# The bias of a decay's exponent: direction 0's inside the exponential, head by head, direction 1's as a difference

## The chip, the cores and the metric

The kernel runs on one core of a Trainium2 chip. The metric is the time of one execution on the device in microseconds (us). Of the core's engines, TensorE (PE) does the matmuls and transposes, VectorE (DVE) the elementwise work on two operands, ScalarE (ACT) functions such as the exponential, GpSimd (POOL) some elementwise work, and the sync engine (SP) issues most of the transfers from memory. Each engine works its own queue of instructions in order.

## The reference, cut to what matters

The layer has two branches behind one input projection: gated linear attention (GLA) and a Mamba-2 scan (SSD), each run in both directions over 512 tokens, merged, and followed by a feed-forward part. The change is in the SSD branch: 32 heads in 4 groups, chunks of 128 tokens. Within a chunk the reference computes for each head

```python
cum = jnp.cumsum(ai, axis=1)
seg = cum[:, :, None] - cum[:, None, :]
Lm = jnp.exp(jnp.where(mask, seg, -jnp.inf))
cb = jnp.einsum('btgn,bsgn->btsg', ci, bi)
y = jnp.einsum('btsg,btsge,bsgep->btgep', cb, Lm, xi)
```

`seg` is the decay's exponent for the pair of tokens t and s, and `xi` is already multiplied by the step size dt. Direction 0 uses the pairs with s at or before t, direction 1 those with s at or after t.

## The kernel before

Each product with weights is made of three matmuls: high part by high part, high by low, low by high. ScalarE writes the high part of a weight tile (`whi_...`, L188) and VectorE the rest (`wlo_...`, L189) from a tile `raw_...` that the sync queue loads (L176).

The SSD branch goes group by group. `ssd_proj(g)` makes B, C, x and the gate z of a group; z comes last, in two halves of 256 columns into banks `r_z` (L386 to L388), and each bank is read by ScalarE (L697) and VectorE (L698) and then used again. `ssd_chain(g)` then runs over the group's four chunks n. The names count chunks (`y_3` is the matmul of chunk 3 of some group); `y_2` in VectorE's rows is the tile of y of group 2. For each chunk and each half of the group's eight heads (`hf`, four heads) the chain makes a tile E of 128 partitions (token s) by 4 x 128 (head, token t), named `E_n_hf_d` in the queue:

- two loads, one for each direction d, bring the row of cumulative sums `cdr` into all partitions (L746). The pool "E4" has four buffers, so two half-chunks are in flight at once.
- VectorE adds `ebias`, which is log dt minus the cumulative sum at s, one value for each partition and head, to each direction (L747).
- `copy_predicated` (L749) writes direction 0's values over direction 1's where s is at or before t.
- ScalarE takes the exponential of the tile (L750), VectorE multiplies it by the product of C and B (L757), and TensorE multiplies it with x into `y_3`.

The pieces of y are then added on VectorE: the contributions `yi` of the two carried states (L773, L774), the bank (L775), the gate z (L776). ScalarE sums the squares (L781), VectorE and GpSimd make the norm's factor (`rv_y`, `rr_y`), VectorE scales (L783). TensorE transposes the result (`yT_3`, L501), ScalarE and VectorE write its high and low part (L788, L789), and `pb` matmuls project it (L632 to L634). While the chain of group g runs, TensorE fills the time with the projections of group g+1, or, for the last group, with the gate projections `l_ga` and `l_gb`.

Nobody writes the order of the queues by hand: a scheduler replays the program by its own estimates of time and writes each engine's queue; matmuls issued through `early` (L501) have priority in it.

Of the kernel before, what the change touches and what calls it, by code (L numbers as in the profile page):

```python
# [11 lines left out]
AF = mybir.ActivationFunctionType  # L12
ALU = mybir.AluOpType

P = 128
# [12 lines left out]
HPG = 8  # L28
# [101 lines left out]
def hybrid_layer_kernel(ctx: ExitStack, tc: tile.TileContext, x, xc, wts, vec, rows, up, msk, lvl, out):  # L130
    nc = tc.nc
# [569 lines left out]
    def ssd_chain(g, bc, bt, xt, z, yH, yL):  # L701
# [35 lines left out]
        for n in range(NCH):  # L737
            tk = slice(n * P, (n + 1) * P)
            EH = HPG // 2
            Eh = []  # L740
            for hf in range(2):
                E = []
                hh = slice(g * HPG + hf * EH, g * HPG + (hf + 1) * EH)
                for d in range(2):
                    ed = ch.tile([P, EH, P], F32, tag="E4", name=f"E_{g}_{n}_{hf}_{d}", bufs=4)
                    nc.sync.dma_start(ed, cdr[d, n, hh, :].unsqueeze(0).to_broadcast([P, EH, P]))  # L746
                    nc.vector.tensor_tensor(ed, ed, ebias[:, d, n, hh].unsqueeze(2).to_broadcast([P, EH, P]), ALU.add)  # L747
                    E.append(ed)
                nc.vector.copy_predicated(E[1], le8.unsqueeze(1).to_broadcast([P, EH, P]), E[0])  # L749
                nc.scalar.activation(E[1], E[1], AF.Exp)  # L750
                Eh.append(E[1])
            pcb = sm_bank(f"cb_{g}_{n}")
            early.matmul(pcb[:, 0:P], bc[:, 0, tk], bc[:, 1, tk], start=True, stop=True)
# [116 lines left out]
    ebias = cst.tile([P, 2, 4, 32], F32, name="ebias")  # L870
    for d in range(2):
        nc.vector.tensor_tensor(ebias[:, d], ldt[:, 0:4, 32 * d:32 * d + 32], cum[:, d], ALU.subtract)
    cdr = dr.tile([2, 4, 32, P], F32, name="cdr")
    for d in range(2):
        pt = sm_bank(f"cumT_{d}")
# [18 lines left out]
    nc.gpsimd.dma_start(ydr, acc_a)  # L894
    yy = back_pair("yT_0")
    ssd_chain(0, *sp, *yy)
    acc_b = ch.tile([P, 8, SEQ], F32, tag="y16", name="acc_b")
    sp = ssd_proj(1)
    proj_back(lambda c: ("pb", 0, c), *yy, acc_b, True)
    yy = back_pair("yT_1")  # L900
    ssd_chain(1, *sp, *yy)
    sp = ssd_proj(2)
    proj_back(lambda c: ("pb", 1, c), *yy, acc_b, False)
    yy = back_pair("yT_2")
    ssd_chain(2, *sp, *yy)
    sp = ssd_proj(3)
    proj_back(lambda c: ("pb", 2, c), *yy, acc_b, False)
# [292 lines left out]
```

## Time and profile before

| | before |
|---|---|
| median of 3 runs | 1412.5 us (1412.01 to 1418.23) |
| profiled execution | 1415.85 us, of which the span in the trace is 1414.1 |
| mean granted clock of TensorE | 0.981 |
| busy: TensorE, VectorE, ScalarE, GpSimd | 1353.3, 871.4, 504.2, 331.7 us |
| chain that ended last | TensorE 80%, VectorE 9%, transfers 6%, ScalarE 2% |

The profiled execution is one of its own and lies 3.35 us above the median. A busy time says how long an engine had work in it; the chain says which work the end of the program waited for.

### The profile page before, as it was taken

Reading aid. Unit: us, or ns where it says so; the run is one execution under the profiler, and the core shown is the slowest. Engines: PE = TensorE matmul, PEld = TensorE weight load, DVE = VectorE, ACT = ScalarE, POOL = GpSimd, SP = SyncE. Lnnn points to the kernel's source line nnn. Section 1 sums busy time; section 2 is a strip of 40 time slices with the busy share of each in tenths; the row PEclk is TensorE's granted clock in tenths of the full one; section 3 lists DMA queues with packets and bytes.
Section 4 is the critical chain, followed back from the end, with each engine's and each line's share of the span. In section 5 each row is a group of like instructions: output and inputs, shape, how many; then the busy total and the mean of one; then the engine's idle time right before and its main releaser. Section 6 shows DMA issues by size and latency. Waiting matters only on the chain.

```text
span 1414.1 us, 19042 instructions
## 1 busy us (share of the span) xinstructions
PE 1353.3 (96%) x7462; PEld 1151.4 (81%) x7462; DVE 871.4 (62%) x1348; ACT 504.2 (36%) x828; POOL 331.7 (23%) x277
## 2 busy tenths in 40 slices
PE   5998999999999999999899989998899999999997
PEld 3797999899889788888878877776688888888886
DVE  4559686573786697678759865777664434332235
ACT  6474343433435232532423342232333232232222
POOL 1355454245001211111021102114641212100001
PEclk9899999999999999999999989999999999999999
DMA  9363322333222333223323233547423343333231
GB/s 367 131 211 105 103 94 94 123 105 123 94 83 90 122 118 103 85 89 93 109 75 103 94 92 96 175 155 252 152 77 119 104 134 120 123 100 104 90 112 67
DMA packets 58010, 169.19 MB, mean 120 GB/s; under 512 B 6064, under 2 KB 10304, under 8 KB 57792
## 3 DMA queue, kind: packets, MB, share of 16 engines
q1 hardware_dynamic: 55328, 157.96, 34.2%
q0 software_dynamic: 2304, 9.64, 2.2%
q8 instruction: 59, 0.97, 0.3%
q10 hardware_dynamic: 288, 0.36, 0.1%
q14 instruction: 31, 0.25, 0.1%
HBM read 156.23 MB, written 11.72 MB: 119 GB/s over the span
## 4 chain that ended last, share of the span: by engine, by line
PE 80%; DVE 9%; DMA 6%; ACT 2%; issue 2%; POOL 1%; SPq 0%; POOLq 0%; DVEq 0%; ACTq 0%
DMA E<-cdr 3%; PE up L1054 3%; PE gate L1053 3%; PE up L1053 3%; PE gate L1054 3%; PE gate L1052 3%; PE up L1052 3%; PE db L204 3%; PE db L206 3%; PE db L205 3%; PE yi L501 2%; PE l_xs L361 2%; PE l_xs L366 2%; PE l_xs L362 2%; PE pb_pb L632 2%; PE pb_pb L633 2%
## 5 line engine op out<-in xcount | busy, mean ns | idle before, releaser
L341 POOL TENSOR_TENSOR raw_ada<-raw_ada,cs 128x1024 f32<-128x1024 f32 x32 | 63.7, 1990 | 277.7 <-DMA raw_ada<-in_wts_dram 234.3
L386 PE MATMUL r_z<-whi_z,hH 128*128 128x256 f32 x256 | 75.6, 295 | 7.4 <-DVE z L698 6.8
L343 POOL TENSOR_TENSOR raw_ada<-raw_ada 128x512 f32<-128x512 f32 x64 | 80.1, 1251 | 4.3
L387 PE MATMUL r_z<-wlo_z,hH 128*128 128x256 f32 x256 | 75.6, 295 | 0.0
L388 PE MATMUL r_z<-whi_z,hL 128*128 128x256 f32 x256 | 74.6, 291 | 0.0
L1052 PE MATMUL gate<-h2H,whi_gate 128*128 128x512 f32 (+1 forms) x192 | 71.6, 373 | 0.3 <-ACT h2H L1023 0.2
L1053 PE MATMUL gate<-h2L,whi_gate 128*128 128x512 f32 (+1 forms) x192 | 71.5, 373 | 0.3 <-DVE h2L L1024 0.3
L747 DVE TENSOR_TENSOR E<-E,ebias 128x512 f32<-128x512 f32 x64 | 46.1, 724 | 41.3 <-DMA E<-cdr 41.0
L1054 PE MATMUL gate<-h2H,wlo_gate 128*128 128x512 f32 (+1 forms) x192 | 71.4, 372 | 0.0
L1054 PE MATMUL up<-h2H,wlo_up 128*128 128x512 f32 x160 | 63.0, 394 | 0.0
L1053 PE MATMUL up<-h2L,whi_up 128*128 128x512 f32 x160 | 62.3, 389 | 0.0
L1052 PE MATMUL up<-h2H,whi_up 128*128 128x512 f32 x160 | 62.2, 389 | 0.0
L189 DVE TENSOR_TENSOR wlo_gate<-raw_gate,whi_gate 128x1024 fp32r<-128x1024 f32 x20 | 33.4, 1672 | 45.2 <-ACT whi_gate L188 45.2
L189 DVE TENSOR_TENSOR wlo_down<-raw_down,whi_down 128x1024 fp32r<-128x1024 f32 x18 | 22.1, 1225 | 62.4 <-ACT whi_down L188 62.3
L386 PEld LDWEIGHTS r_z<-whi_z,hH 128*128 128x128 f32 x256 | 50.7, 198 | 8.4 <-DVE z L698 7.4
L386 PE MATMUL r_v<-whi_v,hH 128*128 128x256 f32 x192 | 55.7, 290 | 1.0 <-ACT whi_v L188 1.0
L205 PE MATMUL db<-wlo_down,fH 128*128 128x512 f32 x142 | 55.2, 389 | 0.0
L206 PE MATMUL db<-whi_down,fL 128*128 128x512 f32 x142 | 55.2, 389 | 0.0
L388 PE MATMUL r_v<-whi_v,hL 128*128 128x256 f32 x192 | 55.1, 287 | 0.0
L632 PE MATMUL pb_pb<-yT,whi_pb 128*128 128x512 f32 x128 | 53.3, 421 | 1.5 <-ACT z L697 1.0
L387 PE MATMUL r_v<-wlo_v,hH 128*128 128x256 f32 x192 | 54.6, 284 | 0.0
L633 PE MATMUL pb_pb<-yT,whi_pb 128*128 128x512 f32 x128 | 52.8, 413 | 1.5 <-DVE yT L789 1.5
(473 smaller groups left out, 4262.6 us busy)
## 6 DMA issues: line engine op xcount, KB each, us to landing
raw_ada<-in_wts_dram SPq DMA_DIRECT2D x32, 512.0 KB, 3.6
E<-cdr SPq DMA_DIRECT2D x64, 256.0 KB, 3.2
raw_gate<-in_wts_dram SPq DMA_DIRECT2D x22, 512.0 KB, 3.6
raw_up<-in_wts_dram SPq DMA_DIRECT2D x22, 512.0 KB, 3.6
raw_down<-in_wts_dram SPq DMA_DIRECT2D x22, 512.0 KB, 3.6
aw<-in_wts_dram SPq DMA_DIRECT2D x8, 1024.0 KB, 15.5
raw_xs<-in_wts_dram SPq DMA_DIRECT2D x16, 512.0 KB, 3.5
raw_z<-in_wts_dram SPq DMA_DIRECT2D x16, 512.0 KB, 3.5
```

Source lines behind the costliest of these rows:

```text
L205: nc.tensor.matmul(out_, aH, bL, start=False, stop=False)
L206: nc.tensor.matmul(out_, aL, bH, start=False, stop=stop)
L341: nc.gpsimd.tensor_tensor(raw, raw, cs[:, :, 0:1].to_broadcast([P, KD, P]), ALU.mult)
L343: nc.gpsimd.tensor_tensor(raw[:, 0:n, :], raw[:, 0:n, :], raw[:, n:2 * n, :], ALU.add)
L386: nc.tensor.matmul(o, hH[:, kk, tk], hi[:, k, :], start=st, stop=False, skip_group_check=True)
L387: nc.tensor.matmul(o, hH[:, kk, tk], lo[:, k, :], start=False, stop=False, skip_group_check=True)
L388: nc.tensor.matmul(o, hL[:, kk, tk], hi[:, k, :], start=False, stop=sp, skip_group_check=True)
L632: nc.tensor.matmul(pt, hi[:, k, cl], aH[:, k, :], start=(k == 0), stop=False)
L633: nc.tensor.matmul(pt, hi[:, k, cl], aL[:, k, :], start=False, stop=False)
L1052: nc.tensor.matmul(pts[kj][:, tk], hi[:, k, :], h2H[:, k, tk], start=(k == 0), stop=False)
L1053: nc.tensor.matmul(pts[kj][:, tk], hi[:, k, :], h2L[:, k, tk], start=False, stop=False)
L1054: nc.tensor.matmul(pts[kj][:, tk], lo[:, k, :], h2H[:, k, tk], start=False, stop=(k == KD - 1))
```

## The change

Direction 0's add is left out. Its bias is put into the exponential instead, where ScalarE can add one value for each partition; as the value differs from head to head, the one instruction over four heads becomes four over one head each. Direction 1's add stays, but adds the difference of the two biases, so that the exponential's bias completes both. The table of differences is made once, after `ebias` is set up.

```diff
--- before.py
+++ after.py
@@ -744,10 +744,13 @@
                 for d in range(2):
                     ed = ch.tile([P, EH, P], F32, tag="E4", name=f"E_{g}_{n}_{hf}_{d}", bufs=4)
                     nc.sync.dma_start(ed, cdr[d, n, hh, :].unsqueeze(0).to_broadcast([P, EH, P]))
-                    nc.vector.tensor_tensor(ed, ed, ebias[:, d, n, hh].unsqueeze(2).to_broadcast([P, EH, P]), ALU.add)
+                    if d == 1:
+                        nc.vector.tensor_tensor(ed, ed, ebias[:, 1, n, hh].unsqueeze(2).to_broadcast([P, EH, P]), ALU.add)
                     E.append(ed)
                 nc.vector.copy_predicated(E[1], le8.unsqueeze(1).to_broadcast([P, EH, P]), E[0])
-                nc.scalar.activation(E[1], E[1], AF.Exp)
+                for e_ in range(EH):
+                    b_ = g * HPG + hf * EH + e_
+                    nc.scalar.activation(E[1][:, e_, :], E[1][:, e_, :], AF.Exp, bias=ebias[:, 0, n, b_:b_ + 1])
                 Eh.append(E[1])
             pcb = sm_bank(f"cb_{g}_{n}")
             early.matmul(pcb[:, 0:P], bc[:, 0, tk], bc[:, 1, tk], start=True, stop=True)
@@ -870,6 +873,8 @@
     ebias = cst.tile([P, 2, 4, 32], F32, name="ebias")
     for d in range(2):
         nc.vector.tensor_tensor(ebias[:, d], ldt[:, 0:4, 32 * d:32 * d + 32], cum[:, d], ALU.subtract)
+
+    nc.vector.tensor_tensor(ebias[:, 1], ebias[:, 1], ebias[:, 0], ALU.subtract)
     cdr = dr.tile([2, 4, 32, P], F32, name="cdr")
     for d in range(2):
         pt = sm_bank(f"cumT_{d}")
```

TensorE keeps its instructions; the scheduler writes all queues anew. Three places follow, each a piece of an engine's queue. A number behind a name only tells tiles of one name apart, `x3` is three alike in a row, and [waits ...] names the engine or transfer queue whose count the instruction waits for (Activation is ScalarE, DMAHW a transfer).

TensorE before, where the chain of group 2 ends and the gate z of group 3 is projected, up to the first `pb` matmul:

```order
L386 MATMUL r_z_1_0_1_7551<-whi_z_1_1_7606,hH 128x256
L387 MATMUL r_z_1_0_1_7551<-wlo_z_1_1_7607,hH 128x256
L388 MATMUL r_z_1_0_1_7551<-whi_z_1_1_7606,hL 128x256
L501 MATMUL yT_3_6988<-idt,y_2_6967 128x128 [waits DVE_49,PE_49]
L501 MATMUL yT_3_6988<-idt,y_2_6967 128x128 x3
L674 MATMUL tr_b_0_7066<-idt,ct_b_7061 128x128 [waits PE_49]
L674 MATMUL tr_b_0_7066<-idt,ct_b_7061 128x128 x3
L674 MATMUL tr_b_1_7072<-idt,ct_b_7061 128x128 [waits PE_49]
L674 MATMUL tr_b_1_7072<-idt,ct_b_7061 128x128
L674 MATMUL tr_x_0_0_7184<-idt,ct_x_0_7181 128x128 [waits PE_49,Activation_49]
L674 MATMUL tr_x_0_0_7184<-idt,ct_x_0_7181 128x128 x3
L632 MATMUL pb_pb_0_0_7674<-yT_6679,whi_pb_0_7668 128x512 [waits Activation_49]
```

TensorE in the change, at the same transposes:

```order
L386 MATMUL r_z_0_0_1_7482<-whi_z_0_1_7537,hH 128x256
L387 MATMUL r_z_0_0_1_7482<-wlo_z_0_1_7538,hH 128x256
L388 MATMUL r_z_0_0_1_7482<-whi_z_0_1_7537,hL 128x256
L501 MATMUL yT_3_7037<-idt,y_2_7016 128x128 [waits DVE_49,PE_49]
L501 MATMUL yT_3_7037<-idt,y_2_7016 128x128 x3
L674 MATMUL tr_b_0_7115<-idt,ct_b_7110 128x128 [waits PE_49]
L674 MATMUL tr_b_0_7115<-idt,ct_b_7110 128x128 x3
L674 MATMUL tr_b_1_7121<-idt,ct_b_7110 128x128 [waits PE_49]
L674 MATMUL tr_b_1_7121<-idt,ct_b_7110 128x128
L674 MATMUL tr_x_0_0_7233<-idt,ct_x_0_7230 128x128 [waits PE_49,Activation_49]
L674 MATMUL tr_x_0_0_7233<-idt,ct_x_0_7230 128x128 x3
L386 MATMUL r_z_1_0_0_7599<-whi_z_1_0_7601,hH 128x256 [waits DVE_49]
```

Before, 48 `r_z` matmuls of the second half of z stand between the last `y_3` and `yT_3`, and `pb` follows the transposes. In the change it is 44 `r_z` of the first half; the second half follows `yT_3` and the transposes, and the first `pb` comes 118 instructions behind `yT_3`. The queue reads the same at the ends of groups 0 and 1, where 64 and 75 instructions stood between the last `y_3` and `yT_3` before; at the end of group 1 the first matmul of the second half (`r_z_1_0_0`) came right behind the last `y_3` and waited for z. At the end of group 3 there are 40 matmuls of 512 columns (`l_ga`, `l_gb`) in that place, and before there were 9.

VectorE before, at the same end of group 2, from the second piece of y to its scaling in L783:

```order
L747 TENSOR_TENSOR E_0_1_1_7858<-E_0_1_1_7858,ebias 128x512 [waits DMAHW6_49]
L774 TENSOR_TENSOR y_2_6967<-y_2_6967,yi_2_6976 128x512 [waits DVE_49]
L749 COPY_PREDICATED E_0_1_1_7858<-le_78,E_0_1_0_7855 128x512 [waits DVE_49]
L775 TENSOR_TENSOR y_2_6967<-y_2_6967,y_3_6958 128x512 [waits DVE_49,PE_49]
L747 TENSOR_TENSOR E_1_0_0_7917<-E_1_0_0_7917,ebias 128x512 [waits DMAHW7_49]
L776 TENSOR_TENSOR y_2_6967<-y_2_6967,z_3_6306 128x512 [waits DVE_49]
L189 TENSOR_TENSOR wlo_pb_0_7669<-raw_pb_0_7670,whi_pb_0_7668 128x1024 [waits Activation_49]
L747 TENSOR_TENSOR E_1_0_1_7920<-E_1_0_1_7920,ebias 128x512 [waits DMAHW0_49]
L168 TENSOR_SCALAR rv_y_6983<-yss_3_6981 128x1 [waits Activation_49]
L698 SCALAR_TENSOR_TENSOR z_3_7431<-z_3_7431,r_z_0_0_1_7433 128x256 [waits DVE_49,Activation_49]
L749 COPY_PREDICATED E_1_0_1_7920<-le_78,E_1_0_0_7917 128x512 [waits DVE_49]
L783 SCALAR_TENSOR_TENSOR y_2_6967<-y_2_6967,rr_y_6985,snw_6680 128x512 [waits Pool_49]
```

VectorE in the change, from the first piece of y to its scaling, which is L786 there (pieces are L776 to L779, the add is L748, the copy L750):

```order
L776 TENSOR_TENSOR yi_2_7020<-yi_3_0_7018,ecum 128x512 [waits PE_49]
L776 TENSOR_TENSOR yi_2_7025<-yi_3_1_7023,ecum 128x512 [waits PE_49]
L777 TENSOR_TENSOR y_2_7016<-y_2_7016,yi_2_7020 128x512 [waits DVE_49,Pool_49]
L777 TENSOR_TENSOR y_2_7016<-y_2_7016,yi_2_7025 128x512 [waits DVE_49]
L778 TENSOR_TENSOR y_2_7016<-y_2_7016,y_3_7007 128x512 [waits DVE_49,PE_49]
L748 TENSOR_TENSOR E_0_1_1_7908<-E_0_1_1_7908,ebias 128x512 [waits DMAHW5_49]
L779 TENSOR_TENSOR y_2_7016<-y_2_7016,z_3_6339 128x512 [waits DVE_49]
L750 COPY_PREDICATED E_0_1_1_7908<-le_78,E_0_1_0_7906 128x512 [waits DMAHW2_49,DVE_49]
L698 SCALAR_TENSOR_TENSOR z_0_7477<-z_0_7477,r_z_0_0_0_7481 128x256 [waits Activation_49]
L168 TENSOR_SCALAR rv_y_7032<-yss_3_7030 128x1 [waits Activation_49]
L786 SCALAR_TENSOR_TENSOR y_2_7016<-y_2_7016,rr_y_7034,snw_6713 128x512 [waits Pool_49]
```

Ahead of y's scaling stand one E add, one copy, one piece of z and `rv_y` now; the add of `E_1_0_0` is gone, and the weight split and the add of `E_1_0_1` come later.

The sync queue before, some way ahead of that place (`raw_` tiles are weights, E tiles the rows of `cdr`):

```order
L746 DMA E_3_0_1_6935<-cdr 128x512 [waits DVE_49]
L746 DMA E_3_1_0_6940<-cdr 128x512 [waits DMAHW5_49,DVE_49]
L176 DMA raw_z_1_1_7608<-in_wts_dram 128x1024 [waits DMAHW6_49,DVE_49]
L176 DMA raw_pb_0_7670<-in_wts_dram 128x1024 [waits DMAHW7_49,DMAHW0_49,DVE_49]
L746 DMA E_3_1_1_6943<-cdr 128x512 [waits DVE_49,PE_49]
L746 DMA E_0_0_0_7847<-cdr 128x512 [waits DMAHW1_49,DVE_49,PE_49]
L746 DMA E_0_0_1_7850<-cdr 128x512 [waits DMAHW2_49,DVE_49]
L176 DMA raw_pb_1_7704<-in_wts_dram 128x1024 [waits DMAHW3_49,DVE_49]
L746 DMA E_0_1_0_7855<-cdr 128x512 [waits DMAHW4_49,DVE_49]
```

The sync queue in the change at the same loads:

```order
L746 DMA E_3_1_0_6987<-cdr 128x512 [waits DMAHW4_49,DMAHW1_49,DVE_49]
L176 DMA raw_z_1_0_7603<-in_wts_dram 128x1024 [waits DMAHW6_49,DVE_49]
L746 DMA E_3_1_1_6989<-cdr 128x512 [waits DVE_49,PE_49]
L746 DMA E_0_0_0_7896<-cdr 128x512 [waits DMAHW7_49,DVE_49,PE_49]
L176 DMA raw_z_1_1_7657<-in_wts_dram 128x1024 [waits DMAHW0_49,DVE_49]
L746 DMA E_0_0_1_7898<-cdr 128x512 [waits DMAHW4_49,DVE_49]
L746 DMA E_0_1_0_7906<-cdr 128x512 [waits DMAHW7_49,DMAHW2_49,DVE_49]
L176 DMA raw_pb_0_7719<-in_wts_dram 128x1024 [waits DMAHW3_49,DVE_49]
L176 DMA raw_pb_1_7753<-in_wts_dram 128x1024 [waits DMAHW5_49,DVE_49]
```

`raw_z_1_1` and `raw_pb_0` now stand behind E loads that stood behind them before.

## Rows read from the trace of the kernel before

**Rows 1.** The page: busy time, share and instructions of TensorE; the chain that ended last.

```profile
PE 1353.3 (96%) x7462; PEld 1151.4 (81%) x7462; DVE 871.4 (62%) x1348; ACT 504.2 (36%) x828; POOL 331.7 (23%) x277
...
PE 80%; DVE 9%; DMA 6%; ACT 2%; issue 2%; POOL 1%; SPq 0%; POOLq 0%; DVEq 0%; ACTq 0%
```

**Rows 2.** Windows: length, busy us (instructions) by engine, TensorE's clock, DMA share, GB/s.

```profile
690.00:825.00 135.00, 129.37 (x739) 110.02 (x740) 100.16 (x164) 44.12 (x77) 19.36 (x17) 0.96 0.27 87
825.00:960.00 135.00, 124.55 (x561) 97.31 (x559) 90.83 (x139) 45.66 (x76) 22.03 (x23) 0.95 0.44 139
```

**Rows 3.** Windows of 10 us, the same columns.

```profile
690.00:700.00 10.00, 7.34 (x42) 7.34 (x43) 4.99 (x10) 4.04 (x9) 0.55 (x1) 0.66 0.22 57
...
810.00:820.00 10.00, 10.00 (x69) 9.52 (x68) 6.10 (x13) 2.33 (x6) 1.05 (x1) 0.83 0.25 79
830.00:840.00 10.00, 7.90 (x28) 6.39 (x29) 6.26 (x10) 5.69 (x11) 0.00 (x0) 0.57 0.50 151
...
960.00:970.00 10.00, 9.79 (x34) 7.94 (x35) 3.66 (x7) 1.74 (x3) 2.19 (x3) 0.78 0.81 290
```

**Rows 4.** Waits of TensorE, 400 to 960 us: total, times, longest.

```profile
PE yT L501 <- DVE y L783: 7.3, 2, 3.8
PE r_z L386 <- DVE z L698: 6.8, 3, 3.3
```

**Rows 5.** TensorE's timeline: start, duration, instruction, [idle before <- releaser].

```profile
562.44 0.39 PE L386 MATMUL r_z<-whi_z,hH 128*128 128x256 f32 x1 [1.58 <-DVE z L698]
562.66 0.28 PE L387 MATMUL r_z<-wlo_z,hH 128*128 128x256 f32 x1
...
692.66 0.58 PE L386 MATMUL r_z<-whi_z,hH 128*128 128x256 f32 x1 [3.27 <-DVE z L698]
693.04 0.41 PE L387 MATMUL r_z<-wlo_z,hH 128*128 128x256 f32 x1
693.26 0.41 PE L388 MATMUL r_z<-whi_z,hL 128*128 128x256 f32 x1
...
830.60 0.63 PE L501 MATMUL yT<-idt,y 128*128 128x128 f32 x4 [3.53 <-DVE y L783]
...
835.48 0.80 PE L633 MATMUL pb_pb<-yT,whi_pb 128*128 128x512 f32 x1 [1.50 <-DVE yT L789]
...
958.43 1.09 PE L501 MATMUL yT<-idt,y 128*128 128x128 f32 x4 [3.76 <-DVE y L783]
```

**Rows 6.** VectorE's timeline at the end of group 2.

```profile
822.93 0.69 DVE L747 TENSOR_TENSOR E<-E,ebias 128x512 f32<-128x512 f32 x1 [1.32 <-DMA E<-cdr]
...
825.36 0.69 DVE L747 TENSOR_TENSOR E<-E,ebias 128x512 f32<-128x512 f32 x1
...
826.59 1.23 DVE L189 TENSOR_TENSOR wlo_pb<-raw_pb,whi_pb 128x1024 fp32r<-128x1024 f32 x1
828.11 0.69 DVE L747 TENSOR_TENSOR E<-E,ebias 128x512 f32<-128x512 f32 x1 [0.28 <-DMA E<-cdr]
...
829.72 0.74 DVE L783 SCALAR_TENSOR_TENSOR y<-y,rr_y,snw 128x512 f32<-128x512 f32 x1
```

**Rows 7.** Groups: L747 (ns min/median/max, waits); ScalarE's, 400 to 960 us (busy, mean ns).

```profile
L747 DVE TENSOR_TENSOR E<-E,ebias x64: 670/693/1277, 412.5 to 934.7; 128x512 f32<-128x512 f32 x64
...
  DMA E<-cdr: 41.0, 39
...
L750 ACT ACTIVATE E<-E 128x512 f32<-128x512 f32 x32 | 20.2, 633 | 80.3 <-DVE E L749 75.6 <-DVE rv_y L168 4.7
...
L657 ACT ACTIVATE cv_x<-c_xs,vecs 128x256 f32<-128x256 f32 x15 | 8.3, 555 | 0.0
...
L675 ACT ACTIVATE x<-tr_x 128x256 f32<-128x256 f32 x16 | 6.2, 386 | 0.0
...
L755 ACT ACTIVATE cbs<-cb 128x128 f32<-128x128 f32 x16 | 4.4, 274 | 26.7 <-PE cb L501 26.7
```

**Rows 8.** Waits of the sync queue, 400 to 960 us.

```profile
SPq L746 <- DVE E L749: 91.9, 27, 6.5
```

## The prediction

> **What bounds the kernel now.** I read the page first: TensorE is busy for 96% of the span and the chain that ended last lies on it for 80%, with 9% on VectorE and 6% on transfers [rows 1]. A change that adds no matmul and takes none away can therefore move the time in two ways only: through the moments in which TensorE stands still, and through the clock at which it runs. So I read next, in two long stretches of the part that the change touches, those of the last two groups, TensorE's busy time and granted clock [rows 2]. From 690 to 825 us it misses 5.6 us of 135 and from 825 to 960 it misses 10.5, at a clock of 0.96 and 0.95. VectorE is busy for two thirds to three quarters of each stretch and ScalarE for a third: neither is full. So the loss sits in short places.
>
> The short windows find the places [rows 3]: four of ten microseconds run at 0.66, 0.83, 0.57 and 0.78. What that costs I take as the missing share of the clock times TensorE's busy time in the window: 0.34 × 7.34 = 2.5, 0.17 × 10 = 1.7, 0.43 × 7.9 = 3.4, 0.22 × 9.79 = 2.2, together 9.8 us. The waits by releaser say for what TensorE stood still from 400 to 960 us: 7.3 us before a `yT` transpose for the scaling of y, 6.8 before an `r_z` matmul for the gate z [rows 4]. The timeline shows them one by one [rows 5]: 3.27 us at 692.66 for z; 3.53 at 830.60 for y and 1.50 at 835.48 for the low half of yT; 3.76 at 958.43 for y. The three z waits sum to 6.8, of which 1.58 is at 562.44 and 3.27 at 692.66, so the third is 1.9; it precedes the window of 0.83. After 692.66 a matmul shows 0.41 us and the next starts 0.22 later; that is the lower of the two clock levels (1.2 instead of 2.4 GHz). After the 1.58 us at 562.44 the next matmul shows 0.28: no fall followed there. At the full clock one `r_z` then takes half of the 0.22, some 0.12 us of the queue. The reader is to see pairs: a stall of some 2 us or more, and a slow stretch behind it that costs nearly as much again.
>
> Why y is late at 830.60, VectorE's timeline says [rows 6]. In its queue, between the first pieces of y and the last (L783, at 829.72 for 0.74 us), stand an E add at 822.93 that waited 1.32 us for its transfer, an add for the next chunk, a weight split `wlo_pb` at 826.59 for 1.23 us, and one more add at 828.11 after another 0.28 of waiting. VectorE works its queue in order, so y pays for all four.
>
> **The change, part by part.** *Removed:* direction 0's add. Of 64 adds of 693 ns median, 32 go [rows 7]: 22 us of VectorE by durations. By itself this is worth nothing, since VectorE has a third to a quarter of its time free; what counts is which of them stand ahead of y or z. *Added at setup:* one subtraction over 128 columns of a small table per partition, once; a quarter of the 693 ns would be 0.17 us, the whole 0.7. TensorE has other work from its queue there, and without that cover it would be under 0.7 us. I take 0.
>
> *ScalarE:* one Exp of 512 columns (633 ns, 32 of them) becomes four of 128 columns with a bias column [rows 7]. The trace has no such instruction. From below stands the 128-column copy with no pointer operand, 274 ns; from above the 256-column one with two pointer operands, 555. That width without pointers takes 386, so one pointer costs about (555 − 386)/2 = 85, and I estimate 274 + 85 = 0.36, with some 0.03 for what reading from SBUF could add, 0.39. Four make 1.56 us for 0.63, so +0.93 each and +30 us in all; the ends are 4 × 0.274 − 0.63 = +0.47 (+15 us) and 4 × 0.555 − 0.63 = +1.6 (+51 us). ScalarE is busy for 44 + 46 = 90 us of the 270 in the two stretches [rows 2], so even the whole +51 would fit into these alone; the cover is its own free time. If it were not covered, the Exp would be ready 0.93 us later, less the 0.6 of the add that went ahead of it: 0.3 us per half. The Trainium skill, "ScalarE: Activation LUTs", section "What ACT_TABLE_LOAD costs", speaks against the split: an instruction with a pointer bias has 280 ns of fixed cost beside 0.833 ns per element, one without has 186, and neighbours overlap by 93. By it four would take 4 × 387 − 3 × 93 = 1.27 us, a sum of about +20 us on ScalarE where mine is +30. No run here shows that instruction.
>
> *Waits:* `copy_predicated` now waits itself for direction 0's transfer, since no add has waited before it. VectorE stood at L747 for 41.0 us in 39 cases [rows 7]; the adds of direction 1 and the copies inherit what of that the transfers cause. Behind that instruction in VectorE's queue stand pieces of y and z, for which TensorE's transposes and `r_z` wait.
>
> *Moved:* the scheduler writes other queues. TensorE's at a group boundary becomes alike in the groups: after the last `y_3` matmul come 44 `r_z`, then `yT_3`, then the whole second half of z, and only then `pb`. Before, in group 2, `yT_3` had 48 `r_z` of the second z half ahead of it and `pb` right behind; in group 1 the second z half came before the z it overwrites was done, the stall at 692.66. In VectorE's queue of group 2, one add, one copy and two small pieces stand between y's parts now, in place of three adds, two copies and the split.
>
> I work this out for 830.60. Of the work ahead of y go the add for `E_1_0_0` (0.69), the split (1.23) and the add for `E_1_0_1` with its wait (0.97): 2.9 us by durations, some 2.7 since neighbours overlap a little. The copy for `E_1_0_1` goes too: it is most of the 0.9 us from the end of that add to L783's start, some 0.6. y ends at 830.46 − 3.3 = 827.2; if the 1.32 us at the remaining add shrink too, at 825.9. TensorE reached `yT_3` at 830.60 − 3.53 = 827.07, and with four `r_z` less (0.12 each) at 826.6. The wait is then 0.6 or nothing; the remaining copy now waits for a transfer itself, as long as 1.3 us if it fares like that add, which makes 1.9 the other end. I take 1.0. The wait of 1.50 for the low half of yT goes, since 0.12 × 48 and more of `r_z` now lie between. The z waits of 3.27 and 1.9 go: `r_z_1_0_0` now stands behind transposes that wait for y, and z's pieces are by y's side in VectorE's queue. But the same boundary in groups 0 and 1 now has 44 `r_z` ahead of `yT_3` where 64 and 75 rows stood, so I put 1.0 us at each too. At the tail of group 3 there were 9 matmuls of 512 columns between `y_3` and `yT_3`, and there are 40 now; a matmul twice as wide as `r_z` at 0.24 us gives 31 × 0.24 = 7.4 us more cover, above the 3.76 us of wait. I leave 1.0 for the split that now stands ahead of the low half of yT.
>
> *Moved past queues:* on the sync queue, `raw_z_1_1` and `raw_pb_1` change places with E loads that wait for buffers. I cost it at nothing: the whole second z half, some 12 us, covers a late `raw_pb`. Without that cover it is the second rival.
>
> **The sum.** Stalls that go: 3.27 + 1.9 + 3.53 + 1.50 + 3.76 = 14.0 us; waits that come: 4 × 1.0 = 4. That is −10. Of the 9.8 us of slow clock I take back 6: stalls of 1 us are below the 1.58 that had no fall behind it, but one of the four may turn out longer. The setup and VectorE's and ScalarE's own sums add 0. So −16 against the profiled execution's 1415.85 us gives 1399.9. That execution lies 3.35 above the median of 1412.5; on the median's scale it is about 1396.5.
>
> **Rivals.** *The waits only move* (27%). For it: 39 waits for E transfers, and the transfers stay, all 64; an add or copy of direction 1 can hold y as well as the one that went; and groups 0 and 1 lose cover, as do the earlier chunks of group 3, whose `l_ga` went to the tail. Against it: less stands ahead of y. Three boundaries of 3.5 us with their slow stretches are then what they were, and the tail alone gains, 3.76 + 2.2 at most: 1406 to 1412, or down to 1404 when one boundary comes out a little better. *Slower: weights come late behind E loads* (13%). The sync queue stood 91.9 us in 27 cases for a buffer that `copy_predicated` frees, 6.5 at the longest [rows 8]. Two such waits ahead of a weight are 13 us, and from 12 on `pb` or `r_z` waits at each of three boundaries. With 3.3 us and 2.5 of slow clock each that is +17.4, against the tail's −6: 1424. Against it: no stall of TensorE above names a transfer. *Nothing left over* (8%): all 14.0 and 9.8 come back, 1388.7. *No effect on TensorE* (5%): what VectorE saves, ScalarE's four Exps give back, and the path of E grows by 0.3 us per half; TensorE's waits are the same, 1412.
>
> **How the numbers follow.** My forecast of 1396.5 has 47%, with a range of its own from 1391 to 1403. A measurement of this kernel tells about 0.5%, 7 us, from no change. Faster than that, below 1405.4, are the forecast, the case in which nothing is left over, and a fifth of the first rival's cases, at its lower end: 0.60. Within it are the rest of that rival and the no-effect case: 0.27. Slower: 0.13. The range of 1387 to 1413 leaves out the slower rival and a little at its lower end.
>
> **What would show it.** Right, if TensorE's waits for y and z from 400 to 960 us, 7.3 + 6.8 before, fall to under 7 together, the windows at the boundaries stay at 1.00, and VectorE's L747 group halves while ScalarE's Exp group reads 128 × 128 at 0.3 to 0.45 us. The prediction is wrong if `yT` still waits above 2 us for y at a boundary, with matmuls of 0.41 behind it, if `r_z` or `pb` wait for a weight split, or if the copy in VectorE's queue waits for E as long as the adds did.

## The result

The change takes 1393.95 us (median of 4 runs, 1392.06 to 1394.12), against 1412.26 for the kernel before in the same comparison (4 runs, 1411.35 to 1418.23). The ratio is 0.986, with a 95% interval of 0.984 to 0.9875: 18.3 us faster. The profiled execution took 1392.06 us, with a span of 1390.3 and a clock of 0.993. Its span is 23.8 us shorter than the one of before; the difference to the 18.3 is that the profiled execution of before lies above its median and that of the change below its own.

The page of the change, in the lines that answer to [rows 1]:

```profile
PE 1339.7 (96%) x7462; PEld 1140.9 (82%) x7462; DVE 854.5 (61%) x1317; ACT 523.5 (38%) x924; POOL 328.0 (24%) x277
...
PE 82%; DVE 7%; DMA 6%; issue 2%; ACT 2%; POOL 2%; SPq 0%; POOLq 0%; DVEq 0%; ACTq 0%
```

TensorE does the same matmuls in 13.6 us less, VectorE has 16.9 us less and ScalarE 19.3 more. In the chain, VectorE's share falls from 9% to 7%. Where TensorE stood from 400 to 960 us, its waits say (total, times, longest), as in [rows 4]:

```profile
PE yT L501 <- DVE y L786: 5.1, 3, 1.7
PE r_z L386 <- DVE cv_x L663: 0.9, 3, 0.3
```

No `r_z` waits for z any more, no `pb` for yT, and the tail (the end of group 3) has no wait at all. The stretch from 400 to 960 us, before and in the change, with the columns of [rows 2]:

```profile
400.00:960.00 560.00, 540.13 (x3009) 452.25 (x3007) 415.66 (x669) 195.06 (x336) 80.48 (x75) 0.98 0.34 108
...
400.00:960.00 560.00, 554.03 (x3111) 464.21 (x3110) 412.12 (x654) 219.35 (x439) 86.99 (x82) 1.00 0.37 120
```

TensorE was busy for 540.13 of 560 us at a clock of 0.98, and is for 554.03 at 1.00. What is left are three alike waits for y, at the ends of groups 0, 1 and 2, in TensorE's timeline:

```profile
559.00 0.63 PE L501 MATMUL yT<-idt,y 128*128 128x128 f32 x4 [1.70 <-DVE y L786]
...
682.44 0.63 PE L501 MATMUL yT<-idt,y 128*128 128x128 f32 x4 [1.71 <-DVE y L786]
...
805.91 0.63 PE L501 MATMUL yT<-idt,y 128*128 128x128 f32 x4 [1.71 <-DVE y L786]
```

None of them has a slow stretch behind it: all ten-microsecond windows from 400 to 960 us read 1.00. Why y is still late there, VectorE's timeline says at the third of them:

```profile
802.03 0.69 DVE L748 TENSOR_TENSOR E<-E,ebias 128x512 f32<-128x512 f32 x1 [1.38 <-DMA E<-cdr]
802.64 0.68 DVE L779 TENSOR_TENSOR y<-y,z 128x512 f32<-128x512 f32 x1
803.24 0.75 DVE L750 COPY_PREDICATED E<-le,E 128x512 f32<-128x512 uint8 x1
803.87 0.41 DVE L698 SCALAR_TENSOR_TENSOR z<-z,r_z 128x256 f32<-128x256 f32 x1
804.20 0.15 DVE L168 TENSOR_SCALAR rv_y<-yss 128x1 f32<-128x1 f32 x1
805.01 0.75 DVE L786 SCALAR_TENSOR_TENSOR y<-y,rr_y,snw 128x512 f32<-128x512 f32 x1 [0.66 <-POOL rr_y L170]
```

The one E add that stayed ahead of y waits 1.38 us for its transfer, as the one in [rows 6] did (1.32), and at the end y waits 0.66 us for GpSimd. Between stand the addition of the gate z to y (L779), a copy and a z piece, as the order had it; the copy doesn't wait, and it and the z piece run beside ScalarE's step on y. From that addition to its scaling y goes through ScalarE's sum of squares (L784), `rv_y` and GpSimd's `rr_y`, in the timelines of these two engines:

```profile
803.44 0.60 ACT L784 ACTIVATE y<-y 128x512 f32<-128x512 f32 x1 [1.70 <-DVE y L779]
...
804.43 0.54 POOL L170 TENSOR_TENSOR rr_y<-rv_y,negh 128x1 f32<-128x1 f32 x1 [8.88 <-DVE rv_y L168]
```

A part of the gain is given back behind the chain. Three points of the two programs, by the first and last starts in TensorE's groups and the span:

| | last `pb` of group 3 | first `hT` | end of the span |
|---|---|---|---|
| before | 983.4 | 1033.1 | 1414.1 |
| the change | 955.7 | 1008.6 | 1390.3 |
| difference | −27.7 | −24.5 | −23.8 |

Of the 27.7 us, 2.0 had come ahead of the chain that was changed: the first `l_xs` starts at 378.75 us, and at 380.73 before. No run shows why. The merge gives back 3.2 us up to the first `hT`. TensorE waits there longer for the weight split of the output projection, before and in the change:

```profile
PE ob L205 <- DVE wlo_out L189: 0.9, 1, 0.9
...
PE ob L205 <- DVE wlo_out L189: 4.8, 3, 2.4
```

Another 0.7 us goes behind the first `hT`, where TensorE waits for the normed rows, with a slow stretch behind it:

```profile
1014.78 1.97 PE L1025 MATMUL hT<-idt,hn 128*128 128x128 f32 x8 [4.44 <-DVE hn L1022]
1016.59 0.58 PE L1057 MATMUL gate<-h2H,whi_gate 128*128 128x256 f32 x1
1016.96 0.41 PE L1057 MATMUL up<-h2H,w_up 128*128 128x256 f32 x1
1017.18 0.41 PE L1057 MATMUL gate<-h2H,whi_gate 128*128 128x256 f32 x1
```

### The profile page after: what moved, and what is told of

Same layout as the page of the kernel before. It is cut to its first block, busy times and chain, and to the rows that moved or that the text cites. A ratio compares the mean times of both kernels' runs of the same rounds, so it can differ in the third digit from the quotient of the medians.

```text
span 1390.3 us, 19141 instructions
## 1 busy us (share of the span) xinstructions
PE 1339.7 (96%) x7462; PEld 1140.9 (82%) x7462; DVE 854.5 (61%) x1317; ACT 523.5 (38%) x924; POOL 328.0 (24%) x277
## 4 chain that ended last, share of the span: by engine, by line
PE 82%; DVE 7%; DMA 6%; issue 2%; ACT 2%; POOL 2%; SPq 0%; POOLq 0%; DVEq 0%; ACTq 0%
PE up L1059 3%; PE gate L1058 3%; PE up L1058 3%; PE gate L1059 3%; PE gate L1057 3%; PE up L1057 3%; PE db L204 3%; PE db L205 3%; PE db L206 3%; DMA E<-cdr 2%; PE yi L501 2%; PE r_z L386 2%; PE r_z L388 2%; PE r_z L387 2%; PE l_xs L361 2%; PE pb_pb L633 2%
## 5 line engine op out<-in xcount | busy, mean ns | idle before, releaser
L341 POOL TENSOR_TENSOR raw_ada<-raw_ada,cs 128x1024 f32<-128x1024 f32 x32 | 66.9, 2090 | 279.0 <-DMA raw_ada<-in_wts_dram 233.1
L387 PE MATMUL r_z<-wlo_z,hH 128*128 128x256 f32 x256 | 72.8, 285 | 0.0
L753 ACT ACTIVATE E<-E,ebias 128x128 f32<-128x128 f32 x128 | 41.2, 391 | 65.1 <-DVE E L750 65.1
L632 PE MATMUL pb_pb<-yT,whi_pb 128*128 128x512 f32 x128 | 54.2, 425 | 0.0
L1066 DVE TENSOR_TENSOR f<-f,up 128x512 f32<-128x512 f32 x22 | 15.1, 687 | 63.1 <-PE up L1059 62.5
L188 ACT ACTIVATE whi_gate<-raw_gate 128x1024 fp32r<-128x1024 f32 x22 | 23.3, 1060 | 76.7 <-PE gate L1058 67.2
```

The costliest lines, as they stand in the source:

```text
L341: nc.gpsimd.tensor_tensor(raw, raw, cs[:, :, 0:1].to_broadcast([P, KD, P]), ALU.mult)
L387: nc.tensor.matmul(o, hH[:, kk, tk], lo[:, k, :], start=False, stop=False, skip_group_check=True)
L632: nc.tensor.matmul(pt, hi[:, k, cl], aH[:, k, :], start=(k == 0), stop=False)
```

## The experiments

Theory A: VectorE's 32 adds less are what counts. They take work from in front of y and z in VectorE's queue, and the scheduler, which counts them too, places `yT_3` and the second half of z so that TensorE has cover. Its rivals: the split of the exponential brought the gain by the order it leads to (B); the split costs time and the missing add pays for it (C); the path of E (load, add, copy, exponential, product, one after another) is what counts, not VectorE. All runs of a comparison stand beside runs of the kernel before; "cover" is the number of matmuls between `y_3` and `yT_3` at the ends of groups 0, 1, 2, and at the tail (before: 64, 75, 48, 9; the change: 44, 44, 44, 40, with the first half of z ahead of `yT_3`).

| run | cover | time, us | ratio to before (95%) |
|---|---|---|---|
| the change | 44, 44, 44, 40 | 1393.95 | 0.984 to 0.9875 |
| e1 split alone | 76, 48, 48, 9 | 1429.08 | 1.009 to 1.016 |
| e2 add left out, one exponential | 66, 46, 46, 47 | 1394.68 | 0.985 to 0.9895 |
| e3 direction 0's add on GpSimd | 66, 46, 46, 47 | 1401.07 | 0.989 to 0.994 |
| e4 add back off E's path | 76, 48, 52, 6 | 1413.61 | 0.999 to 1.002 |
| e5 z's splits on GpSimd | 59, 66, 64, 6 | 1432.4 | 1.012 to 1.015 |
| e6 8 adds back | 64, 80, 30, 11 | 1418.18 | 1.0025 to 1.005 |
| e7 both adds on GpSimd | 66, 73, 77, 44 | 1397.42 | 0.988 to 0.991 |
| e8 the change, pb's splits on GpSimd | 44, 44, 66, 32 | 1400.12 | 0.990 to 0.9925 |
| e9 16 adds back | 43, 43, 43, 35 | 1408.06 | 0.995 to 0.9975 |
| e10 4 adds back | 69, 76, 57, 10 | 1414.99 | 1.000 to 1.003 |
| e11 the change, chunk 0's add on GpSimd | 62, 66, 51, 40 | 1398.18 | 0.987 to 0.991 |
| e12 16 operations back, no extra tile | 43, 43, 43, 35 | 1400.51 | 0.989 to 0.993 |

**e1, the split alone**

```diff
-                nc.scalar.activation(E[1], E[1], AF.Exp)
+                for e_ in range(EH):
+                    nc.scalar.activation(E[1][:, e_, :], E[1][:, e_, :], AF.Exp, bias=zer[:, 0:1])
```

> Both adds stay on VectorE; only the exponential is split into four of 128 columns, each with a bias column of zeros. Theory A (what counts is VectorE's 32 adds less, which takes work from in front of y and z and lets the queues close up): no gain, the stalls of TensorE for y and z stay above 12 us in 400 to 960 us, and the time is within 0.5% of before, 1407 to 1419. Theory B (the split itself, by the order of the queues that it leads to, brought the gain): 1390 to 1400. Theory C (the split costs, and the missing add has to pay for it): above 1419, ScalarE some 21 us busier and Exp late ahead of the product with C B.

Measured: 1429.08 us, 15 slower than before. Theory B falls. The time is that of C, but a part of it comes from something else, the tile of zeros `zer` (by e9 and e12 an estimated 7.5 us, without which the time is still C's). The waits of TensorE in 400 to 960 us, and the group of the exponentials:

```profile
PE yT L503 <- DVE y L786: 16.9, 4, 6.5
PE r_z L388 <- DVE z L700: 4.3, 2, 2.2
...
L753 ACT ACTIVATE E<-E,zer x128: 386/390/408, 411.5 to 938.8; 128x128 f32<-128x128 f32 x128
```

y is up to 6.5 us late. ScalarE's four take 1.29 us together at 827.43 in its timeline where one took 0.63.

**e2, the add left out**

```diff
-                    nc.vector.tensor_tensor(ed, ed, ebias[:, d, n, hh]...)
+                    if d == 1:
+                        nc.vector.tensor_tensor(ed, ed, ebias[:, d, n, hh]...)
```

> Direction 0's add is left out and nothing takes its place (the bias of direction 0 is missing from the output); one exponential of 512 columns as before. Theory A: all of the gain, 1387 to 1398, and the same order at the ends of the groups as in the change. Theory B: 1407 to 1419. Theory C: better than the change by what the split costs, 1380 to 1390.

Measured: 1394.68 us, as the change. So the adds bring all of the gain, and the split, with the adds gone, costs nothing that can be seen: C falls too, as a statement on the change. With VectorE as full as before, in e1, it isn't free.

**e3, direction 0's add on GpSimd**

```diff
-                    nc.vector.tensor_tensor(ed, ed, ebias[:, d, n, hh]...)
+                    (nc.vector if d else nc.gpsimd).tensor_tensor(ed, ed, ebias[:, d, n, hh]...)
```

> Direction 0's add goes from VectorE to GpSimd; the exponential is one, as before, and the output is the reference's. Theory A: as good as the change, 1388 to 1400, since VectorE loses the same 32 adds. If it is the path of E that counts (add, copy, exponential, one after another), no gain: GpSimd's add is slower than the 0.69 us of VectorE's, so 1405 to 1420. If GpSimd slows VectorE down, VectorE's operations of 512 columns grow above 0.69 us.

Measured: 1401.07 us: two thirds of the gain, though the add is slower (1277 ns in the mean). The path of E isn't what decides. Nor is it VectorE's busy time by itself: that is 872.8 us, and was 871.4 before with the 32 adds [rows 1]. The cover is that of e2.

**e4, the add put back where nobody waits for it**

```diff
                 nc.vector.copy_predicated(E[1], le8..., E[0])
+                nc.vector.tensor_tensor(E[0], E[0], ebias[:, 1, n, hh]..., ALU.add)
```

> The change, with one more VectorE add per half of a chunk on the tile of direction 0 after the copy has read it (its result is used by nobody). VectorE has 64 adds again, but the path of E is that of the change. Theory A: most of the gain goes, 1403 to 1416, with stalls for y or z of 2 us or more at the ends of groups. If the path of E counts: the gain stays, 1391 to 1398.

Measured: 1413.61 us; the whole gain is gone, with the path of E that of the change. The dead add also keeps direction 0's buffer longer, but that hardly makes E late: VectorE's waits for E transfers from 400 to 960 us are 28.8 us, and 25.3 in the change. TensorE's waits from 400 to 960 us are those of before again, for y and for z:

```profile
PE yT L501 <- DVE y L787: 9.6, 3, 4.7
PE r_z L386 <- DVE z L698: 6.0, 4, 2.5
```

**e5, other work taken from VectorE**

```diff
-            (nc.gpsimd if split_pool[0] else nc.vector).tensor_tensor(lo, ...)
+            (nc.gpsimd if split_pool[0] or key[0] in ('z',) else nc.vector).tensor_tensor(lo, ...)
```

> The kernel before, with the 16 low-part splits of the z weights on GpSimd and not on VectorE: VectorE loses 16 x 1.23 = 20 us, as much as by the change, and the output is the reference's. All 64 adds stay. The scheduler leaves the queues in the order of before: 59, 66 and 64 matmuls between the last y_3 and yT_3, and 6 at the tail. If VectorE's load is what counts: 1390 to 1402. If the order of the queues is what counts (theory A as sharpened by the runs so far): stalls of TensorE for y and z as before, and 1405 to 1418. A split on GpSimd takes longer; if that is what decides, TensorE's waits name wlo_z.

Measured: 1432.4 us, 19.6 slower. It doesn't tell load from order as meant, because VectorE wasn't freed: over the whole run it is busy for 881.7 us, and was for 871.4 [rows 1]. (A fixed stretch doesn't show it: from 400 to 960 us it is 413.05 here and 412.12 in the change, which has got further by then.) Its operations grew while GpSimd's splits ran (ns: shortest, median, longest):

```profile
L747 DVE TENSOR_TENSOR E<-E,ebias x64: 668/691/2861, 412.6 to 943.8; 128x512 f32<-128x512 f32 x64
...
L189 POOL TENSOR_TENSOR wlo_z<-raw_z,whi_z x16: 2346/2394/2882, 412.7 to 824.5; 128x1024 fp32r<-128x1024 f32 x16
```

An E add takes up to 2861 ns there, against 1277 at the longest in [rows 7].

**e6, 8 adds back**: the change, with the add (of a tile of zeros) for `d == 0` where `n == 0`.

> The change, with direction 0's add (of zeros) put back for the first chunk of each group only, 8 of the 32. VectorE has 5 us more than in the change. The order of the queues falls back to that of before: 64, 80 and 30 matmuls ahead of yT_3, 11 at the tail. By the load alone: 1394 to 1399. By the order: most of the gain goes, 1402 to 1416, with stalls at the end of group 2 and at the tail.

Measured: 1418.18 us. 5 us of VectorE's work and the tile of zeros (an estimated 7.5 us, see e12) cost 24 us, and the waits for z are back (10.1 us in 4 from 380 to 1060 us).

**e7, both adds on GpSimd, and e8, the change with the splits of `pb` on GpSimd.** e7 writes `nc.gpsimd` for the add of L747, e8 has `('pb',)` in e5's line.

> The kernel before, with both adds on GpSimd, one exponential: VectorE loses all 64 adds (44 us), GpSimd gets 64 x 1.28 = 82 us, the output is the reference's. The order has 66, 73 and 77 matmuls ahead of yT_3 and no E add in VectorE's queue ahead of y, 44 matmuls at the tail. If freeing VectorE is what counts, better than the change: 1385 to 1393. If GpSimd becomes late for E, TensorE waits for y_3 or y, and 1398 to 1412.

> The change, with the low-part splits of the pb weights on GpSimd: VectorE loses another 16 x 1.23 us. The order at groups 0 and 1 is that of the change (44), group 2 has 66, the tail 32. If the order is kept the time is that of the change, 1390 to 1397, since no such split stands ahead of y there; below 1390 if VectorE's load still limits. If the slower split is late, TensorE waits for wlo_pb, and 1397 to 1405.

Measured: 1397.42 and 1400.12 us. In e7 y is late by 0.5 us in all, but `tr_x` waits 4.8 us for VectorE's `ct_x`; VectorE is busy for 852.9 us in all, 18.5 less than before, though 64 adds of 46.1 us together have left it: its other operations grew, the 32 copies of E alone from 735 to 1131 ns in the mean. In e8 y is still late (3.6 us in 3), and `pb` waits 1.0 us once for its split. Neither beats the change.

**e9, e10 and e12: load against order.** Which adds are put back decides whether the scheduler keeps the order of the change. e9 puts 16 back and keeps it; e10 puts 4 back and loses it.

```diff
-                    if d == 1:
-                        nc.vector.tensor_tensor(ed, ed, ebias[:, 1, n, hh]...)
+                    if d == 1 or (n, hf) in ((0, 1), (1, 1), (2, 0), (3, 1)):    # e10: (n, hf) == (1, 0)
+                        eb = ebias[:, 1, n, hh] if d == 1 else zer[:, 0:EH]
+                        nc.vector.tensor_tensor(ed, ed, eb..., ALU.add)
```

> The change, with 16 of the 32 adds of direction 0 (of zeros) put back on VectorE, at the halves (n, hf) = (0,1), (1,1), (2,0) and (3,1) of each group. With these the scheduler keeps the order of the change: 43, 43 and 43 matmuls ahead of yT_3 and 35 at the tail. VectorE has 16 x 0.69 = 11 us more. If the load of VectorE decides: half of the gain goes, some 1403. If the order decides: 1392 to 1398.

> The change, with only 4 of the 32 adds (of zeros) put back, at (n, hf) = (1,0) of each group, 2.8 us for VectorE. With these the order turns to that of before: 69, 76 and 57 matmuls ahead of yT_3 with the second half of z in front of it, 10 at the tail, and the next chunk's add ahead of y. If the load decides: 1394 to 1397. If the order decides: 1404 to 1420, as the 8 adds put back before gave 1418.

Measured: 1408.06 and 1414.99 us. e10 is as the order has it: 2.8 us of work cost 21. e9 is outside of both forecasts. Stage by stage, as in the table above (last `pb`, first `hT`, end): 964.8, 1017.4, 1406.3 for e9, 969.1, 1026.7, 1412.4 for e10. From the first `hT` on, e9 takes 388.9 us and e10 385.7, where before takes 381.0 and the change 381.7. The groups of the feed-forward part, 1060 to 1260 us, show why (busy us, mean ns), in e9 and in the change:

```profile
L1060 PE MATMUL gate<-h2H,whi_gate 128*128 128x512 f32 x143 | 56.6, 395 | 0.0
...
L1061 PE MATMUL up<-h2L,whi_up 128*128 128x512 f32 x141 | 55.7, 395 | 0.0
```

```profile
L1058 PE MATMUL up<-h2L,whi_up 128*128 128x512 f32 x148 | 57.6, 389 | 0.0
...
L1057 PE MATMUL gate<-h2H,whi_gate 128*128 128x512 f32 x144 | 56.0, 389 | 0.0
```

The same matmuls, those of `gate` and `up`, take 395 ns and not 389, at the full clock. It is so in e1, e6, e9 and e10, the runs that hold the tile of zeros `zer`, and in no other. So e12 puts back 16 operations at the places of e9 without it:

```diff
                     if d == 1:
                         nc.vector.tensor_tensor(ed, ed, ebias[:, 1, n, hh]..., ALU.add)
+                    elif (n, hf) in ((0, 1), (1, 1), (2, 0), (3, 1)):
+                        nc.vector.tensor_tensor(ed, ed, ed, ALU.max)
```

> The same 16 VectorE operations as in the run before with 16 adds put back, at the same places and with the same order of the queues, but as the maximum of the tile with itself, so that no tile of zeros is needed. In the four runs with that tile (the split alone and the three with adds put back) the 512-column matmuls of the feed-forward part showed 395 ns and in all others 389, some 6 us over 960 of them. If the tile's place in memory is the cause: 389 ns again, and 1400 to 1403. If the load of VectorE brought that too: 395 ns and 1406 to 1410. If the order alone decides, once the tile is gone: 1392 to 1398; if load and order both count: 1399 to 1404, with TensorE's waits for y at 2.1 to 2.7 us and slow clock behind some of them.

Measured: 1400.51 us, and 389 ns in the feed-forward part; its points are 963.3, 1018.3 and 1397.9. That is the case in which load and order both count. With the order kept, 16 operations on VectorE cost 6.6 us, as y is later at the ends of groups 1 and 2, with a slow stretch (0.83 from 810 to 820 us) behind the third wait:

```profile
560.26 0.63 PE L501 MATMUL yT<-idt,y 128*128 128x128 f32 x4 [1.62 <-DVE y L788]
...
684.91 0.63 PE L501 MATMUL yT<-idt,y 128*128 128x128 f32 x4 [2.54 <-DVE y L788]
...
810.96 1.08 PE L501 MATMUL yT<-idt,y 128*128 128x128 f32 x4 [2.99 <-DVE y L788]
```

What makes y late at the third is still the E add ahead of it, which waits longer for its transfer than in the change (2.54 us, 1.38 there). Why that transfer lands later was not followed. In VectorE's timeline:

```profile
807.09 0.69 DVE L748 TENSOR_TENSOR E<-E,ebias 128x512 f32<-128x512 f32 x1 [2.54 <-DMA E<-cdr]
```

With the order lost, 4 adds cost 21 us. The tile's share in that is an estimate: e9 takes 7.5 us more than e12 with the same places and the same cover, and 6 ns on the 960 matmuls of `gate` and `up` are 5.8 of them. That leaves some 13.5 us for the 4 adds. In the chain alone, to the last `pb`, e10 is 13.4 us behind the change and e12 7.6; the tile is not quite out of that either, since the last group's `l_ga` and `l_gb` take 115.6 us in e9 and 114.2 in e12.

**e11, direction 1's add of the first chunk on GpSimd**

```diff
-                        nc.vector.tensor_tensor(ed, ed, ebias[:, 1, n, hh]...)
+                        (nc.gpsimd if n == 0 else nc.vector).tensor_tensor(ed, ed, ebias[:, 1, n, hh]...)
```

> The change, with direction 1's add of the first chunk of each group (8 of 32) on GpSimd, so that no E add stands in VectorE's queue between the pieces of y at the end of a group. The order has 62, 66 and 51 matmuls ahead of yT_3, first half of z first, and 40 at the tail; the output is the reference's. If the 3 x 1.7 us that TensorE still waits for y come from that add's wait for its transfer, they go, and the time is 1386 to 1392. If GpSimd's add makes the copy late, the wait stays and it is 1392 to 1399.

Measured: 1398.18 us, 4 slower than the change. The waits for y go as meant but for 0.7 us, and others come:

```profile
PE tr_x L674 <- DVE ct_x L667: 2.7, 2, 1.8
PE r_z L386 <- DVE z L698: 2.6, 1, 2.6
PE yT L501 <- DVE y L786: 0.7, 1, 0.7
```

## Why the prediction was right, step by step

The forecast was 1396.5 us with its own range from 1391 to 1403, and 1393.95 was measured. The mechanism is the one named: stalls of TensorE for y and z at the ends of the groups, and the clock behind them.

- *Stalls.* 14.0 us were to go and 4.0 to come. All that were named went [rows 5]; 5.1 came, three at 1.7 and none at the tail. Net −8.9 where −10 was forecast. The 1.0 for each boundary was too small because y's path was mis-sized: the working took off 3.3 us, the durations of all that no longer stands ahead of y. But 2.7 of them stood behind the addition of z, largely in the shadow of ScalarE's and GpSimd's steps. From the start of that addition to y's end it took 4.50 us before, and takes 3.12 in the change (802.64 to 805.76):

```profile
825.96 0.69 DVE L776 TENSOR_TENSOR y<-y,z 128x512 f32<-128x512 f32 x1
...
829.72 0.74 DVE L783 SCALAR_TENSOR_TENSOR y<-y,rr_y,snw 128x512 f32<-128x512 f32 x1
```

So 1.4 us came of those 2.7. With 1.3 us less taken off, the 0.6 of the working becomes 1.9, and 1.7 was measured. The upper end of 1.9 in the text had another reason, a copy that waits, and the copy doesn't. The tail's 1.0 was too much.
- *Clock.* 6 of the 9.8 us were to come back. The windows of [rows 3] all read 1.00 in the same places of the change, so all 9.8 did. The pairing of long stalls with slow stretches held at both ends only: waits of 1.70 and 1.71 us have none behind them, as the 1.58 of [rows 5] had none, while the 4.44 at 1014.78 has one. Between, it goes both ways: the clock stayed at 1.00 behind 2.39 us at 971.18 of the change and 2.54 at 684.91 of e12, and fell behind 1.86 at 809.02 of e2 (0.68 from 810 to 815 us). That none of the three 1.7 us was followed by a slow stretch was a narrow thing.
- *Not in the sum:* smaller waits of the stretch (19.9 us idle in all before, 6.0 now) went along, some 5 us more than the ones that were named. So did two slow windows that were not counted, 0.92 from 840 to 850 us and 0.88 from 950 to 960, by the prediction's formula 1.5 us. 2.0 us had come ahead of the chain, and the merge and what follows give back 3.9.
- *The number.* The sum was made on the scale of the profiled execution, and there −16 stands against −23.8 measured. That the median moved by only 18.3 and landed 2.5 us from the forecast is in part luck: the profiled execution of before is 3.6 us above its median, and the terms that were left out go both ways.
- *VectorE.* −22 us was forecast; the page shows −16.9, and in the merge operations like those of the last section below grew (the four on `mt` from 4.2 to 8.2 us). The removed add was said to be worth nothing by itself and to count for what stands ahead of y and z. e4 and e12 bear that out: an add whose result nobody uses costs as much as one that is needed, and 16 operations cost 6.6 us even where the order stays.
- *ScalarE.* 0.39 us was estimated for one Exp of 128 columns with a bias column, and 388 ns is the median:

```profile
L753 ACT ACTIVATE E<-E,ebias x128: 384/388/407, 413.7 to 910.1; 128x128 f32<-128x128 f32 x128
```

Four were put at 1.56 us by leaving out the overlap; they take 1.26 at 804.07 in ScalarE's timeline (1.29 in e1), so 30 us on ScalarE was too much and the page's +19.3 is what it came to. The Trainium skill, "ScalarE: Activation LUTs", section "What ACT_TABLE_LOAD costs", gave 387 ns and 1.27 us for four, some +20 us: the trace agrees. That its fixed cost would speak against the split is not borne out in the change, where ScalarE has the time.

The rivals: *the waits only move* has its place in the three 1.7 us, most of which (1.38) is the remaining add's wait for its transfer, but not its price. The copy inherited no wait: VectorE's waits for E transfers fell from 41.0 us in 39 [rows 7] to 25.3 in 23, all at the add. *Weights late* did not come: no wait of TensorE up to the merge names a weight. *No effect* is refuted by the time and by TensorE's waits; e2 adds that the split gives nothing back that can be seen.

One thing the forecast took as given that the runs had to show: that the order is part of the effect. How large a part was not shown, since no run has all 32 operations back in the order of the change: 16 of them cost 6.6 us with that order, and 4 that overturn it an estimated 13.5. The order of the change is one that 4 adds at one place overturn (e10) and 16 at others don't (e12), so the 18.3 us are not what 32 adds are worth in general. Why the scheduler turns at these places was not looked into and stays open.

## What to carry to other kernels

When TensorE is nearly full, look for its few long waits and the slow stretches behind them, and ask what stands ahead of the late operand in the queue of the engine that makes it; an engine with a quarter of its time free can still be the one that is late. Where a scheduler writes the queues, a few microseconds of work more or less can turn the order at every repeat of a loop and move the time by several times as much (2.8 us of adds by some 13.5 here, an estimate): compare the orders before the times, and don't credit the edit alone. Don't add a helper tile to an experiment without comparing the stages that it should not touch.

## What the runs showed of the hardware

**VectorE beside GpSimd.** In the merge of the change, VectorE's timeline has an addition of one column that takes 1.85 us, where it took 0.14 us at 1008.56. GpSimd's timeline has a weight split around it:

```profile
1000.02 1.85 DVE L1017 TENSOR_TENSOR hs<-hss 128x1 f32<-128x1 f32 x1 [0.81 <-ACT o L1014]
...
1008.56 0.14 DVE L1017 TENSOR_TENSOR hs<-hss 128x1 f32<-128x1 f32 x1
```

```profile
999.46 2.39 POOL L189 TENSOR_TENSOR wlo_gate<-raw_gate,whi_gate 128x1024 fp32r<-128x1024 f32 x1
```

Both end at 1001.85 to 1001.87. It is much the same for e5's longest add: it takes 2.86 us from 794.81, a split on GpSimd runs from 794.72 for 2.40, and the add ends 0.55 us behind it. The Trainium skill, "SBUF — State Buffer", section "SBUF: two separate sides", says that of a VectorE operation with two inputs from SBUF and a GpSimd operation that reads SBUF, the one that starts first holds a shared port pair for its whole instruction, and the other one blocks. The trace agrees: in both cases GpSimd had started first. None of the runs that moved work from VectorE to GpSimd (e3, e5, e7, e8, e11) beat the change; that this is the reason in each of them was not shown apart.

**A small tile slows matmuls elsewhere.** With 4 or 16 bytes for each partition more in the pool of constants, the 512-column matmuls of `gate` and `up` took 395 ns for 389, and those of `l_gb<-hL` in the last group 395 for 390 (e9 and e12). Not all are touched: `db<-whi_down` shows 389 in both. That it comes with the tile and not with the operations or the order is shown by e9 and e12, and by e1, in which ScalarE reads the tile and not VectorE. That it does so by moving the operands' addresses is a guess, and was not tried.
